# Hybrid decoder layer: operands of the recurrence through device memory, one forward substitution per head pair, low parts of weights on VectorE

## The chip, the cores and the metric

One core of a Trainium2 chip runs the program. The metric is the device time of one execution in microseconds; times given are medians of several executions. The engines are TensorE (PE in the profile; its weight loads are PEld), VectorE (DVE), ScalarE (ACT), GpSimd (POOL) and SyncE (SP), whose queue issues most DMAs. Each engine takes its instructions in the order of the program for that engine and waits on semaphores for the others.

## The reference

The layer takes x (1024 tokens, width 1024) through a SwiGLU feed-forward, a token mixer, a second feed-forward and a gated embedding, with layer norms between. Only the token mixer matters here, and of it the RWKV-7 half (512 columns, 8 heads of 64), which is a recurrence over the tokens:

```python
def _rwkv7_scan(r, w, k, v, kk, a):
    b_vec = kk * a
    def step(state, inp):
        r_t, w_t, k_t, v_t, kk_t, b_t = inp
        sa = jnp.einsum('bhvk,bhk->bhv', state, kk_t)
        state = (state * w_t[:, :, None, :] - sa[..., None] * b_t[:, :, None, :]
                 + v_t[..., None] * k_t[:, :, None, :])
        return state, jnp.einsum('bhvk,bhk->bhv', state, r_t)
    ...

def _token_mixer(hin, w_in, ...):
    z = jnp.einsum('bsd,dc->bsc', hin, w_in)
    z_ret, z_rw = z[..., :RET_COLS], z[..., RET_COLS:]
    ...
    ret = _retention_chunkwise(q, k, v)
    ret_out = jax.nn.silu(g) * _head_group_norm(ret, ret_gn_g, ret_gn_b, RET_GN_EPS)
    ...
    y = _rwkv7_scan(r_h, decay, k_h, v_h, kk, a)
    rw_out = (_head_group_norm(y, rw_gn_g, rw_gn_b, RWKV_GN_EPS) + bonus) * gate
    mixed = jnp.concatenate([ret_out, rw_out], axis=-1)
    return jnp.einsum('bsc,cd->bsd', mixed, w_out)
```

All of it is float32; large products are done as three products of split operands (a high part and a low part, `split`, lines 46 to 48, and `mm3`, lines 61 to 63).

## The kernel before

The mixer computes z in 31 column tiles of 128 (three of them before the stage, 28 in it: `z_tile`, 48 z products of 128x512 each, 1344 in all), stores them in device memory and takes the recurrence in chunks of 128 tokens. A unit is a pair of heads (u) and a half of the tokens (h): 8 units, each of 4 chunks of both heads, so 8 matrices of 128x128. For every unit:

- `rw_inputs` mixes neighbouring tokens, computes decays and the normalised key. On TensorE these are the products `wpw`, `apw`, `sspw`, `rnpw` and `bnpw`, on VectorE and ScalarE a chain between them.
- `rw_operands` (line 986) makes the operands `ar`, `bb`, `kp` and the matrices M1 (products `m1pw`, masked copies on line 1003), and the transposed `vt`, `bt`, `kt`. All of them stay in SBUF, in two buffers each.
- `substitution` (line 1015) inverts the 32 diagonal blocks of 32x32 of the unit: the matrices are written to device memory (1021), the blocks read back with a block per partition (1025, 32 partitions), and 31 steps of a product (1033) and a sum (1035) on VectorE work on all blocks at once. The result is written out (1037).
- `doublings` (line 1039) reads it back into the diagonal of `Xd` (1045), transposes it on VectorE (1047), and makes the inverse of 128x128 from it with the products `i1w` (1056) to `i5w`.
- `rw_chunks` runs the four chunks one after another: score products `scpw` (1099, 1102), masked copies on VectorE (1107, 1108), the products `chw` with two ScalarE copies between them, and the new state `wst` (1135). Then the group norm (`gstw`, `gnyw`, lines 797 to 805) and the output.

`retention` handles the other half of the heads (`vtpr`, `ktpr`, `rspr`, `kvpr`, `yor`). The z products of later pairs, and near the end the output projection (`w_out_group`, products `wopo`, 384 of them), are given as filler at low priority. In `z_tile` the low part of a weight is made on GpSimd (but for the first tile of the stage), in `w_out_operand` on GpSimd for every other operand.

The order of each engine's instructions is settled when the program is built: a list scheduler places them by priority (program order, moved by `high_priority`), so an instruction of low priority goes where its engine would otherwise be free; `issue_after(self.gate)` holds filler back until the matrix products that `gate` names. The loop of steps in `mixer` sets the program order:

```python
            for s in range(-1, 8):
                if s + 1 < 8:
                    self.rw_operands(W[s + 1])
                if s == -1:
                    self.lora(lor, 1)
                if s >= 0:
                    u, h = units[s]
                    self.doublings(W[s])
                    self.rw_chunks(W[s], mixed[4 + u])
                if s + 2 < 8:
                    W[s + 2] = inputs(s + 2)
```

Step s handles unit s; an odd step is the second half of the tokens of a pair.

## Time and profile before

| | us |
|---|---|
| median of 3 executions | 2357.45 (2352.09 to 2362.36) |
| profiled execution | 2365.46, span 2363.3 |
| TensorE busy | 2262.3 (96%) |
| VectorE busy | 1622.9 (69%) |
| ScalarE busy | 842.7 (36%) |
| GpSimd busy | 751.9 (32%) |
| recurrence stage | from 720 to 1564 of the span |
| first doublings of the steps 0 to 7 | 870, 923, 1016, 1078, 1198, 1260, 1379, 1437 |

The profile is of one execution, 8.0 us above the median. Busy time is the union of an engine's instructions; matmuls overlap one another, so a matmul's duration is longer than the distance to the next. "PEclk" is the granted TensorE clock as a share of full speed. Durations below are from this execution.

### The profile page before, as it was taken

What the parts mean: (1) busy time and instruction counts of PE and PEld (TensorE: products, weight loads), DVE (VectorE), ACT (ScalarE), POOL (GpSimd) and SP (SyncE); (2) the same over time, 40 slices, a digit from 0 to 9 for tenths busy, and PEclk for the clock granted to TensorE, in tenths of its full rate; (3) what the DMA queues carried; (4) which work ended last, traced back from release to release, by engine and by line L of the source; (5) the groups of instructions that cost most, each with busy time, mean ns of one, the idle gap of its engine ahead of it and who ended that gap; (6) DMA issues with size and microseconds to landing.
All of it is one profiled execution on the core that took longest, in us unless ns stands there. A gap on an engine that the chain in (4) does not pass through costs nothing.

```text
span 2363.3 us, 30893 instructions
## 1 busy us (share of the span) xinstructions
PE 2262.3 (96%) x10753; PEld 1818.2 (77%) x10753; DVE 1622.9 (69%) x2702; ACT 842.7 (36%) x1430; POOL 751.9 (32%) x614
## 2 busy tenths in 40 slices
PE   6999999999999899999899999988999999999999
PEld 5788888788786677777677777766888788788787
DVE  7677777665782487773864876679676767866862
ACT  4323232344643433322322322264323232445550
POOL 3336454300102323332432423225555453000220
PEclk9999999999999999999999999999999999999999
DMA  4345555497336343323333353322465544974321
GB/s 144 112 155 181 182 179 165 149 337 239 90 133 199 116 124 99 108 79 93 113 92 112 98 175 120 98 89 85 156 196 161 188 159 139 350 257 155 112 76 41
DMA packets 288945, 345.97 MB, mean 146 GB/s; under 512 B 35571, under 2 KB 162134, under 8 KB 288790
## 3 DMA queue, kind: packets, MB, share of 16 engines
q1 hardware_dynamic: 284208, 331.37, 43.6%
q0 software_dynamic: 3328, 12.06, 1.3%
q8 instruction: 85, 1.39, 0.2%
q10 hardware_dynamic: 1254, 0.58, 0.1%
q14 instruction: 70, 0.57, 0.1%
HBM read 237.50 MB, written 106.43 MB: 146 GB/s over the span
## 4 chain that ended last, share of the span: by engine, by line
PE 79%; DVE 14%; issue 2%; ACT 2%; DMA 1%; POOL 1%; SPq 0%; DVEq 0%; ACTq 0%; POOLq 0%
PE f1m L61 6%; PE f1m L62 6%; PE f1m L63 6%; PE f2m L61 5%; PE f2m L63 5%; PE f2m L62 5%; PE z L63 3%; PE z L61 3%; PE z L62 3%; DVE ixw L1035 2%; DVE itw L1033 2%; PE f1qa L62 1%; PE f1qa L61 1%; PE scpw L1099 1%; PE f1qa L63 1%
## 5 line engine op out<-in xcount | busy, mean ns | idle before, releaser
L63 PE MATMUL z<-x1Th,lo_win 128*128 128x512 f32 x448 | 191.3, 427 | 5.3 <-DVE lo_win L48 2.9
L61 PE MATMUL z<-x1Th,hi_win 128*128 128x512 f32 x448 | 191.1, 427 | 0.8 <-ACT hi_win L47 0.8
L62 PE MATMUL z<-x1Tl,hi_win 128*128 128x512 f32 x448 | 187.9, 420 | 0.0
L48 POOL TENSOR_TENSOR lo_win<-raw_win,hi_win 128x512 fp32r<-128x512 f32 x54 | 74.7, 1384 | 160.3 <-ACT hi_win L47 140.3
L1033 DVE TENSOR_TENSOR itw<-iltw,ixw 32x31 f32<-32x31 f32 (+15 forms) x248 | 104.5, 421 | 29.8 <-DMA iltw<-scrw 14.3
L1035 DVE TENSOR_TENSOR ixw<-ixw,itw 32x31 f32<-32x31 f32 (+15 forms) x248 | 108.9, 439 | 4.0
L63 PEld LDWEIGHTS z<-x1Th,lo_win 128*128 128x128 f32 x448 | 87.2, 195 | 26.4 <-POOL lo_win L48 4.0
L61 PEld LDWEIGHTS z<-x1Th,hi_win 128*128 128x128 f32 x448 | 87.5, 195 | 24.2 <-issue 3.8
L62 PEld LDWEIGHTS z<-x1Tl,hi_win 128*128 128x128 f32 x448 | 87.5, 195 | 20.3 <-issue 2.9
L149 POOL TENSOR_TENSOR f2tb<-f2tb,f2tb 128x512 f32<-128x512 f32 x44 | 71.9, 1634 | 91.5 <-DMA f2tb<-in_ffn_w_down 83.6
L48 DVE TENSOR_TENSOR f1hl<-f1s,f1hh 128x512 fp32r<-128x512 f32 x63 | 45.5, 723 | 61.6 <-ACT f1hh L47 61.6
L149 POOL TENSOR_TENSOR f1tb<-f1tb,f1tb 128x512 f32<-128x512 f32 x44 | 66.5, 1511 | 42.2 <-DMA f1tb<-in_ffn_w_down 35.7
L48 DVE TENSOR_TENSOR f2hl<-f2s,f2hh 128x512 fp32r<-128x512 f32 x63 | 44.8, 711 | 44.9 <-ACT f2hh L47 44.9
L47 ACT CAST f1hh<-f1s 128x512 fp32r<-128x512 f32 x63 | 39.2, 622 | 92.1 <-PE f1qa L62 42.3
L47 ACT CAST f2hh<-f2s 128x512 fp32r<-128x512 f32 x63 | 39.2, 623 | 89.8 <-PE f2qa L62 36.1
L659 ACT COPY zs<-z 128x512 f32<-128x512 f32 x56 | 32.7, 583 | 97.2 <-PE z L63 84.9
L108 DVE TENSOR_TENSOR f2S<-f2w 128x512 f32<-128x512 f32 x22 | 17.5, 800 | 72.1 <-DMA f2w<-in_ffn_w_gu 67.3
L47 ACT CAST hi_win<-raw_win 128x512 fp32r<-128x512 f32 x56 | 34.6, 619 | 90.2 <-PE z L62 82.2
L48 POOL TENSOR_TENSOR f1A12l<-f1w,f1A12h 128x512 fp32r<-128x512 f32 x22 | 30.9, 1408 | 106.8 <-ACT f1A12h L47 106.8
L62 PE MATMUL f2qa<-f2vl,f2hh 128*128 128x512 f32 x164 | 63.9, 390 | 0.5 <-DVE f2vl L48 0.5
L62 PE MATMUL f1qa<-f1vl,f1hh 128*128 128x512 f32 x164 | 63.9, 389 | 0.0
L63 PE MATMUL f2qa<-f2vh,f2hl 128*128 128x512 f32 x164 | 63.8, 389 | 0.0
(785 smaller groups left out, 7197.9 us busy)
## 6 DMA issues: line engine op xcount, KB each, us to landing
f1w<-in_ffn_w_gu SPq DMA_DIRECT2D x44, 512.0 KB
f2w<-in_ffn_w_gu SPq DMA_DIRECT2D x44, 512.0 KB
f1s<-hd SPq DMA_DIRECT2D x63, 256.0 KB
f2s<-hd SPq DMA_DIRECT2D x63, 256.0 KB
zs<-zs SPq DMA_DIRECT2D x56, 256.0 KB
raw_win<-in_w_in SPq DMA_DIRECT2D x54, 256.0 KB
f1tb<-in_ffn_w_down SPq DMA_DIRECT2D x44, 256.0 KB
wt<-f1tb SPq DMA_DIRECT2D x44, 256.0 KB
```

The source lines that it names most:

```text
L47: self.last_split = self.nc.scalar.copy(hi, src).ins
L48: (eng or self.nc.vector).tensor_tensor(out=lo, in0=src, in1=hi, op=ALU.subtract)
L61: mm(ps, a[0], b[0], start=first, stop=False)
L62: mm(ps, a[0], b[1], start=False, stop=False)
L63: mm(ps, a[1], b[0], start=False, stop=last)
L108: sub = lambda o, a, b, op=ALU.subtract: V.tensor_tensor(out=o, in0=a, in1=b, op=op)
L149: nc.gpsimd.tensor_tensor(out=t, in0=a, in1=b, op=ALU.subtract)
L659: nc.scalar.copy(zs, ps)
L1033: nc.vector.tensor_tensor(out=t, in0=lt[:, j, j + 1:].unsqueeze(2).broadcast_to([B, n, c]), in1=x[:, j:j + 1, 0:c].broadcast_to([B, n, c]) ...
L1035: nc.vector.tensor_tensor(out=x[:, j + 1:, 0:c], in0=x[:, j + 1:, 0:c], in1=t, op=ALU.add)
L1099: nc.tensor.matmul(ps[e][:, 0:2 * P], kp[rr, cs], ar[rr, c].rearrange("p a t -> p (a t)"), start=True, stop=True)
```

## The change

The operands of a unit (`ar`, `bb`, `kp`, `vt`, `bt`, `kt`) are written to a tensor in device memory, three of them by SyncE's queue and three by ScalarE's, and `rw_chunks` reads them back with one DMA for each chunk (448 KB, four buffers). The tiles in SBUF in which they are made, and M1, are single now; M1 is read back from device memory for the doublings. `substitution` takes the two units that follow an odd step (or both first units at the start) at once, 64 blocks on 64 partitions, and is called after the doublings of that odd step and before its chunks. `rw_inputs` and `rw_operands` of unit s + 2 come at the head of step s. The low parts of the weights of z and of the output projection are all made on VectorE.

```diff
@@ rw_operands
-        w.M1 = self.M1[w.h]
+        w.ops = self.dpool.tile([P, 4, 7, P], F32, tag="ops", name=f"ops{nm}", bufs=5)
+        w.L = self.dpool.tile([P, 8, P], F32, tag="scr", name=f"scr{nm}", bufs=5)
+        T = lambda tag, shape=[HALF], bufs=1: mb.tile([P] + shape, F32, tag=tag, name=f"{tag}{nm}", bufs=bufs)
...
-        self.substitution(w)
+        nc.sync.dma_start(w.L, self.M1)
...
-        toks = []
-        for t, x in (("vt", w.v), ("bt", w.bb), ("kt", w.kp)):
+        nc.sync.dma_start(w.ops[:, :, 2], c4(w.bb))
+        nc.sync.dma_start(w.ops[:, :, 0:2], w.ar)
+        nc.sync.dma_start(w.ops[:, :, 3], c4(w.kp))
+        for i, (t, x) in enumerate((("vt", w.v), ("bt", w.bb), ("kt", w.kp))):
             o = T("w" + t)
             nc.scalar.copy(o, self.transposes(x, f"{t}p{nm}"))
-            toks.append(o)
-        w.vt, w.bt, w.kt = toks
+            nc.scalar.dma_start(w.ops[:, :, 4 + i], c4(o))
@@ substitution
-    def substitution(self, w):
+    def substitution(self, ws):
...
-        scr = self.dpool.tile([P, 8, P], F32, tag="scr", name=f"scr{nm}", bufs=2)
-        nc.sync.dma_start(scr, w.M1)
-        lt = mb.tile([B, B, B], F32, tag="ilt", name=f"ilt{nm}", bufs=1)
-        for b in range(4):
-            bs = slice(B * b, B * b + B)
-            nc.sync.dma_start(lt[8 * b:8 * b + 8], scr[bs, :, bs].rearrange("i s j -> s i j"))
+        n_ = B * len(ws)
+        lt = mb.tile([n_, B, B], F32, tag="ilt", name=f"ilt{nm}", bufs=1)
+        for i, w in enumerate(ws):
+            for b in range(4):
+                bs = slice(B * b, B * b + B)
+                nc.sync.dma_start(lt[B * i + 8 * b:B * i + 8 * b + 8], w.L[bs, :, bs].rearrange("i s j -> s i j"))
...
-            nc.vector.tensor_tensor(out=t, in0=lt[:, j, j + 1:].unsqueeze(2).broadcast_to([B, n, c]),
-                              in1=x[:, j:j + 1, 0:c].broadcast_to([B, n, c]), op=ALU.mult)
+            nc.vector.tensor_tensor(out=t, in0=lt[:, j, j + 1:].unsqueeze(2).broadcast_to([n_, n, c]),
+                              in1=x[:, j:j + 1, 0:c].broadcast_to([n_, n, c]), op=ALU.mult)
             nc.vector.tensor_tensor(out=x[:, j + 1:, 0:c], in0=x[:, j + 1:, 0:c], in1=t, op=ALU.add)
...
@@ doublings
+        M1 = mb.tile([P, 8, P], F32, tag="M1", name=f"M1{nm}", bufs=1)
+        nc.sync.dma_start(M1, w.L)
@@ rw_chunks, for each chunk c
+            o = mb.tile([P, 7, P], F32, tag="ops", name=f"ops{nm}{c}", bufs=4)
+            nc.sync.dma_start(o, w.ops[:, c])
+            ar, (bb, kp, vt, bt, kt) = o[:, 0:2], [o[:, i] for i in range(2, 7)]
@@ w_out_operand
-            self.split(*parts, raw, self.nc.gpsimd if i else self.nc.vector)
+            self.split(*parts, raw)
@@ mixer
-                    self.z_tile(x1T, c0, zs[idx[c0]], *((nc.scalar, nc.vector) if early else (nc.sync, nc.gpsimd)))
+                    self.z_tile(x1T, c0, zs[idx[c0]], nc.scalar if early else nc.sync, nc.vector)
...
-                if s + 1 < 8:
-                    self.rw_operands(W[s + 1])
                 if s == -1:
+                    self.rw_operands(W[0])
                     self.lora(lor, 1)
+                if 0 < s + 2 < 8:
+                    W[s + 2] = inputs(s + 2)
+                    self.rw_operands(W[s + 2])
                 if s >= 0:
                     u, h = units[s]
                     self.doublings(W[s])
+                if s % 2 and s + 2 < 8:
+                    self.substitution([W[s + 1], W[s + 2]])
+                if s >= 0:
                     self.rw_chunks(W[s], mixed[4 + u])
-                if s + 2 < 8:
-                    W[s + 2] = inputs(s + 2)
```

Two places show what this does to the order of the engines.

TensorE at the start of the stage, the products of the second unit's inputs: before, z products (filler, lines 61 to 63) follow the last product of the decays, `apw`; 17 z products later comes `sspw` and then, with z products between them, `rnpw`, `bnpw` and `m1pw`.

```order
L931 MATMUL wpw_1_6870<-lor0w_1_6847,lorww_1_6849 128x512
L933 MATMUL apw_1_6872<-lor0w_1_6847,lorww_1_6849 128x512
L61 MATMUL z_0_6938<-x1Th,hi_win_0_6928 128x512
L62 MATMUL z_0_6938<-x1Tl_3698,hi_win_0_6928 128x512
L63 MATMUL z_0_6938<-x1Th,lo_win_0_6929 128x512
L61 MATMUL z_0_6938<-x1Th,hi_win_0_6928 128x512
L62 MATMUL z_0_6938<-x1Tl_3699,hi_win_0_6928 128x512
L63 MATMUL z_0_6938<-x1Th,lo_win_0_6929 128x512
```

The same place after (`gps` are the last gate products of `lora`):

```order
L782 MATMUL gps_1_6743<-ld_1_6715,gupzk_6721 128x512
L933 MATMUL apw_1_6774<-lor0w_1_6749,lorww_1_6751 128x512
L965 MATMUL sspw_1_6803<-ones,sqw_1_6801 128x2 x4
L812 MATMUL rnpw_1_6814<-ident,rbw_1_6812 128x128 x4
L980 MATMUL bnpw_1_6824<-rkw_1_6822,ones 128x512
L1001 MATMUL m1pw_10_6835<-arw_1_6830,bbw_1_6832 128x128 x3
L1001 MATMUL m1pw_11_6836<-arw_1_6830,bbw_1_6832 128x128 x3
L1001 MATMUL m1pw_10_6835<-arw_1_6830,bbw_1_6832 128x128
L1001 MATMUL m1pw_11_6836<-arw_1_6830,bbw_1_6832 128x128
L61 MATMUL z_0_6997<-x1Th,hi_win_0_6987 128x512
```

The z products have moved behind the whole chain. Up to the first `i1w` of the stage 432 z products stand in the order before and 370 after; 192 and 130 of them come after `apw`.

VectorE, before, in the chunks of step 0: the substitution of the next unit (`itw`, `ixw`) alternates with the masked copies of the scores (`scz`) and the state (`wst`).

```order
L1107 COPY_PREDICATED scz_6353<-mask,scpw_010_9093 128x256
L1033 TENSOR_TENSOR itw_115_8926<-iltw_1_8873,ixw_1_8878 32x256
L1108 COPY_PREDICATED scz_6353<-mask,scpw_010_9093 128x128
L1035 TENSOR_TENSOR ixw_1_8878<-ixw_1_8878,itw_115_8926 32x16x16
L1131 TENSOR_SCALAR wst_6361<-chw_00_9075,few_0_7682 64x64
L1033 TENSOR_TENSOR itw_116_8929<-iltw_1_8873,ixw_1_8878 32x255
L1131 TENSOR_SCALAR wst_6361<-chw_00_9075,few_0_7682 64x64
L1035 TENSOR_TENSOR ixw_1_8878<-ixw_1_8878,itw_116_8929 32x15x17
```

After, at the end of the chunks of step 1, where the substitution of units 2 and 3 begins (the steps have lines 1035 and 1037 now):

```order
L1144 SCALAR_TENSOR_TENSOR wst_6359<-chw_12_8392,few_1_6794,sfw_121_8407 64x64
L797 TENSOR_REDUCE gstw_1_8444<-yrw_1_8305 128x8
L798 TENSOR_SCALAR gstw_1_8444<-gstw_1_8444 128x8
L799 TENSOR_TENSOR gnyw_1_8445<-yrw_1_8305,gstw_1_8444 128x512
L802 TENSOR_REDUCE gstw_1_8444<-gsqw_1_8449 128x8
L804 RECIPROCAL gstw_1_8444<-gstw_1_8444 128x8
L805 TENSOR_TENSOR gnyw_1_8445<-gnyw_1_8445,gstw_1_8444 128x512
L1035 TENSOR_TENSOR itw_00_8210<-iltw_0_8198,ixw_0_8207 64x31
L1037 TENSOR_TENSOR ixw_0_8207<-ixw_0_8207,itw_00_8210 64x31
L1035 TENSOR_TENSOR itw_01_8213<-iltw_0_8198,ixw_0_8207 64x60
L1037 TENSOR_TENSOR ixw_0_8207<-ixw_0_8207,itw_01_8213 64x30x2
```

The steps stand behind the chunks and the group norm of an odd step, and nothing of them stands in the chunks of any step. On TensorE, 136 z products stood between the last chunk of each of the steps 1, 3 and 5 and the next `i1w`; now there are 139, 150 and 134, and the products `m1pw` of the next unit (and, in steps 3 and 5, `sspw`, `rnpw` and `bnpw`) have left this stretch for the chunks.

## Rows read from the trace of the kernel before

**Rows 1.** Stage windows: length, busy PE, PEld, DVE, ACT, POOL, PEclk, DMA share, GB/s.

```profile
720.00:870.30 150.30, 136.51 (x560) 97.90 (x559) 68.60 (x135) 57.69 (x93) 46.97 (x63) 0.97 0.47 146
870.30:1564.00 693.70, 660.09 (x3706) 519.87 (x3704) 480.46 (x1075) 207.03 (x398) 233.94 (x226) 0.96 0.35 108
```

**Rows 2.** Windows of the three stretches after an odd step's last chunk.

```profile
964.50:1015.80 51.30, 47.98 (x234) 38.08 (x234) 39.43 (x95) 15.81 (x27) 18.70 (x17) 0.93 0.48 143
1138.50:1197.80 59.30, 52.70 (x250) 41.32 (x249) 44.46 (x89) 19.49 (x34) 28.14 (x22) 0.91 0.39 117
1321.40:1379.10 57.70, 51.67 (x248) 41.44 (x247) 45.08 (x89) 17.90 (x31) 28.11 (x21) 0.91 0.40 117
```

**Rows 3.** Windows of two even steps.

```profile
1015.80:1077.90 62.10, 57.72 (x327) 45.93 (x326) 44.67 (x105) 17.92 (x38) 26.31 (x26) 0.95 0.26 78
1197.80:1259.80 62.00, 57.58 (x334) 45.05 (x333) 47.57 (x106) 16.86 (x36) 26.28 (x28) 0.97 0.33 99
```

**Rows 4.** Groups of the substitution: count, busy us, mean ns, idle before.

```profile
L1033 DVE TENSOR_TENSOR itw<-iltw,ixw 32x31 f32<-32x31 f32 (+15 forms) x248 | 104.5, 421 | 29.8 <-DMA iltw<-scrw 14.3 <-POOL csw L941 11.7
L1035 DVE TENSOR_TENSOR ixw<-ixw,itw 32x31 f32<-32x31 f32 (+15 forms) x248 | 108.9, 439 | 4.0
```

**Rows 5.** Timeline, step 3's tail: start us, us, engine, line, operation.

```profile
1151.30 0.41 DVE L1035 TENSOR_TENSOR ixw<-ixw,itw 32x256 f32<-32x256 f32 x1
1151.46 2.00 POOL L975 TENSOR_TENSOR wkw<-wkw,kfw 128x512 f32<-128x512 f32 x1 [3.12 <-DVE kkw L974]
1152.24 1.50 DVE L1033 TENSOR_TENSOR itw<-iltw,ixw 32x255 f32<-32x255 f32 x1
```

**Rows 6.** Timeline, from step 1's last chunk to step 2's first doubling.

```profile
964.22 0.39 PE L1143 MATMUL chw<-saw,scz 128*128 128x64 f32 x2
1005.01 0.18 DVE L1035 TENSOR_TENSOR ixw<-ixw,itw 32x31 f32<-32x31 f32 x1
1005.40 0.32 SPq L1037 DMA_DIRECT2D scsw<-ixw  x1
1007.59 1.78 SPq L1045 DMA_DIRECT2D Xd<-scsw  x4
1015.53 0.39 PE L63 MATMUL z<-x1Th,lo_win 128*128 128x512 f32 x1
1015.76 0.94 PE L1056 MATMUL i1w<-Xd,M 128*128 128x128 f32 x7
```

**Rows 7.** Timeline, the second unit's inputs.

```profile
808.16 0.69 PE L933 MATMUL apw<-lor0w,lorww 64*128 64x512 f32 x1
815.08 1.05 PE L965 MATMUL sspw<-ones,sqw 128*128 128x2 f32 x8 [1.63 <-ACT sqw L962]
824.43 1.46 PE L980 MATMUL bnpw<-rkw,ones 128*128 128x512 f32 x2 [2.13 <-DVE rkw L978]
829.78 0.72 DVE L1003 COPY_PREDICATED M<-mask,m1pw 128x512 f32<-128x512 uint8 x1
```

**Rows 8.** Timeline, SyncE queue between first unit's matrix and its substitution.

```profile
801.09 0.33 SPq L1021 DMA_DIRECT2D scrw<-M  x1
804.75 1.51 SPq L1025 DMA_DIRECT2D iltw<-scrw  x4
```

**Rows 9.** Source line L1056, first step: duration ns, first and last start.

```profile
L1056 PE MATMUL i1w<-Xd,M x16: 272/275/275, 870.6 to 872.2; 128*128 128x128 f32 x16
```

**Rows 10.** Source line L48 in the stage, GpSimd and VectorE.

```profile
L48 POOL TENSOR_TENSOR lo_win<-raw_win,hi_win x54: 1256/1294/3362, 735.1 to 1377.7; 128x512 fp32r<-128x512 f32 x54
L48 POOL TENSOR_TENSOR mw<-wo,mw x16: 1263/1293/1730, 1410.3 to 1542.7; 128x512 fp32r<-128x512 f32 x16
L48 DVE TENSOR_TENSOR lo_win<-raw_win,hi_win x2: 673/677/681, 720.7 to 725.8; 128x512 fp32r<-128x512 f32 x2
```

**Rows 11.** Timeline, a DMA issued by ScalarE.

```profile
705.49 0.41 ACTq L52 DMA_DIRECT2D raw_win<-in_w_in  x1
```

**Rows 12.** DMA issues: KB each, median us to landing.

```profile
x<-xacc POOLq DMA_DIRECT2D x8, 512.0 KB, 2.9
```

More of the change, by code (lines that the diff above doesn't have):

```diff
@@ L714, in mixer_setup @@
         nc.vector.tensor_copy(self.mask, m.rearrange("p (a b) -> p a b", a=2))
-        self.M1 = [c.tile([P, 8, P], F32, name=f"M1{i}") for i in range(2)]
+        self.M1 = c.tile([P, 8, P], F32, name="M1")
         self.Xd = c.tile([P, 8, P], F32, name="Xd")
-        for t in self.M1 + [self.Xd]:
+        for t in (self.M1, self.Xd):
             nc.gpsimd.memset(t, 0.0)
@@ L1055, in doublings @@
             for i in range(4):
-                nc.tensor.matmul(ps[:, i * P:(i + 1) * P], w.M1[:, 4 * q + i], self.Xd[:, 4 * q + i], start=True, stop=True)
+                nc.tensor.matmul(ps[:, i * P:(i + 1) * P], M1[:, 4 * q + i], self.Xd[:, 4 * q + i], start=True, stop=True)
             pm = mb.tile([P, 4, P], F32, tag="ipm", name=f"ipm{nm}{q}", bufs=2)
@@ L1071, in doublings @@
         for i in range(8):
-            nc.tensor.matmul(ps[hi, 64 * i:64 * i + 64], w.M1[lo, i, hi], X64[lo, i], start=True, stop=True)
+            nc.tensor.matmul(ps[hi, 64 * i:64 * i + 64], M1[lo, i, hi], X64[lo, i], start=True, stop=True)
         pm = mb.tile([P, 8, 64], F32, tag="ipm", name=f"ipn{nm}", bufs=2)
@@ L1084, in rw_chunks @@
         sl = slice(h * HALF, (h + 1) * HALF)
-        ar, bb, kp, vt, bt, kt, XT, fe = w.ar, w.bb, w.kp, w.vt, w.bt, w.kt, w.XT, w.fe
+        XT, fe = w.XT, w.fe
         yr = self.ring("c", f"yr{nm}")
@@ L1098, in rw_chunks @@
                 rr = slice(64 * e, 64 * e + 64)
-                nc.tensor.matmul(ps[e][:, 0:2 * P], kp[rr, cs], ar[rr, c].rearrange("p a t -> p (a t)"), start=True, stop=True)
+                nc.tensor.matmul(ps[e][:, 0:2 * P], kp[rr], ar[rr].rearrange("p a t -> p (a t)"), start=True, stop=True)
             for e in range(2):
                 rr = slice(64 * e, 64 * e + 64)
-                nc.tensor.matmul(ps[e][:, 2 * P:3 * P], bb[rr, cs], ar[rr, c, 1], start=True, stop=True)
+                nc.tensor.matmul(ps[e][:, 2 * P:3 * P], bb[rr], ar[rr, 1], start=True, stop=True)
             E = []
@@ L1112, in rw_chunks @@
             if not first:
-                nc.tensor.matmul(ch[:, 0:P], ar[:, c, 0], st, start=True, stop=False)
+                nc.tensor.matmul(ch[:, 0:P], ar[:, 0], st, start=True, stop=False)
             for e in range(2):
-                vs = slice(c * P + 64 * e, c * P + 64 * e + 64)
+                vs = slice(64 * e, 64 * e + 64)
                 nc.tensor.matmul(ch[:, 64 * e:64 * e + 64], E[e][:, 0], vt[:, vs], start=first, stop=first or e == 1)
@@ L1124, in rw_chunks @@
             if not (h == 1 and c == 3):
-                nc.tensor.matmul(ch[:, 2 * P:3 * P], kt[:, cs], vt[:, cs], start=True, stop=False)
-                nc.tensor.matmul(ch[:, 2 * P:3 * P], bt[:, cs], sa, start=False, stop=True)
+                nc.tensor.matmul(ch[:, 2 * P:3 * P], kt, vt, start=True, stop=False)
+                nc.tensor.matmul(ch[:, 2 * P:3 * P], bt, sa, start=False, stop=True)
                 for e in range(2):
@@ L1137, in rw_chunks @@
             if not first:
-                nc.tensor.matmul(ch[:, Y:], ar[:, c, 1], st, start=True, stop=False)
+                nc.tensor.matmul(ch[:, Y:], ar[:, 1], st, start=True, stop=False)
             for e in range(2):
-                vs = slice(c * P + 64 * e, c * P + 64 * e + 64)
+                vs = slice(64 * e, 64 * e + 64)
                 es = slice(Y + 64 * e, Y + 64 * e + 64)
```

21 lines of the change are left out of this document (11 added, 10 removed).

## The prediction

> **What bounds the kernel now.** First the table of stages. The change touches the recurrence stage alone, from 720 to 1564 us. In its eight steps (870.3 to 1564) TensorE is busy 660.1 of 693.7 us, VectorE 480.5, GpSimd 233.9, ScalarE 207.0, DMA 0.35 [rows 1]: TensorE bounds it, idle for 33.6 us, and its granted clock of 0.96 takes another 0.04 x 693.7 = 28 us. So 61 us of these steps are stall and 632 are work at full clock.
>
> Then the same table by step, to see where the stall lies. The "tail" of an odd step runs from its last chunk to the next step's first doubling. The three tails that have a next substitution in them last 51.3, 59.3 and 57.7 us, with 3.3, 6.6 and 6.0 idle and clocks of 0.93, 0.91 and 0.91 that cost 3.6, 5.3 and 5.2: 30.0 us of stall, half of all, over 44.4 + 47.4 + 46.5 = 138.3 us of work [rows 2]. Two even steps show 7.5 and 6.3 us of stall by the same sum [rows 3]. In the second and third tail VectorE is busy 44.5 and 45.1 us, and the timeline shows what with: substitution steps, with everything else of VectorE between them. TensorE goes in order, so a tail lasts as long as the longer of two things: its own queued work, and VectorE's way to the first doubling's operand.
>
> **The change part by part.**
>
> *Four substitutions instead of eight.* One has 62 instructions and takes (104.5 + 108.9) / 8 = 26.7 us [rows 4]; four fewer take 106.7 us from VectorE. The new ones have 64 partitions and as many elements on each. I take the same duration, since an instruction of 128 partitions and 512 elements takes 0.68 us [rows 10] and the longest step, 32 x 256, 0.41 [rows 5]; the other end, twice the time, would leave VectorE where it is. Undisturbed, a step takes 0.18 (shortest) to 0.41 us (longest) [rows 5, 6], some 20.3 us for 62; so 6.4 us of 26.7 are disturbance. One step shows it: 1.50 us instead of 0.41 while GpSimd multiplies [rows 5].
>
> The Trainium skill, page "SBUF — State Buffer", section "SBUF: two separate sides", says that VectorE and GpSimd share a port pair as an exclusive lock, held for a whole instruction. The trace agrees: that step grew by 1.1 us beside a 2.00 us product.
>
> *The start.* In the new order of TensorE nothing stands between the second unit's input products and its matrix; the z products that filled this stretch come after. The matrix must now be there before the one substitution can begin. In the trace the chain from the `apw` product (808.2) to the copied matrix (830.5) takes 22.3 us [rows 7], with substitution steps and a z copy in it; without them I take 18, between 16 (up to the last input product, 824.4) and 22. Then: matrix out and blocks back, 801.1 to 806.3, and 2 to land, 7 us [rows 8]; the run, 20.3 and some 6.5 of other work between (four low parts of 0.68, z products' rotation, mixing), 27 us; out and back again 6.3 us (write issued 1005.4, reads issued until 1009.4, and 2.2 to land as the write took) [rows 6]. From 809.5 this ends at 868, where the first doubling stands at 870.6 now [rows 9]. But 130 z products lie before it in place of 192, and each takes 0.23 us [rows 6]: 62 x 0.23 = 14.3 us of work is left for later, less 2.8 for the earlier doubling: **+11.5 us**, between +8 and +17.
>
> *The tails.* No chunk has substitution steps in it any longer; the whole run stands in the odd tail, behind the group norm. Today's way in the first tail: last chunk product ends at 964.6, last substitution step at 1005.2, operand back at 1011.6, so 47.0 us [rows 6] (TensorE came to the doubling only at 1015.8, having z products to do). New in it: the seven shortest steps, which stood before the tail (+1.6), four low parts (+2.7), the group norm ahead of the run instead of among it (+2.6, an estimate: four passes of 0.67). Gone: two matrix copies of 0.72 [rows 7], and half of the disturbance, since GpSimd loses its low parts (-3.2). That gives 49; a wait of VectorE for the retention products should shrink too, so I take 48, between 43 (no disturbance, waits gone) and 53 (all added, none gone). TensorE's own tail work: the z products go from 136 each to 139, 150 and 134 (+3.5 us), the matrix products and three transposes move into the chunks (16 + 12 instructions at 0.107 [rows 9], 3.0 us per tail), and in two tails the products of the next inputs (2.2 us: 1.05 for the sums of squares [rows 7], the rest alike). So 42.1, 45.4 and 40.8 us of work: all below 48. The tails take 144 instead of 168.3 us, -24.3; the 10.0 us of work that left them is done in the chunks: **-14.3 us**.
>
> *Chains of the inputs* now run among the doublings and chunks of all steps. Today they cost 7.5 and 6.3 in even steps [rows 3] and little in odd chunks, which are full of z products. I take 3 to 4 us for each of six, as much as goes: **0**, between -8 and +8.
>
> *Operands through device memory.* Per unit SyncE issues eight DMAs more (three operands, four chunk loads, the matrix) at 0.32 us [rows 6], 2.6 us in a queue in which z stores and weight loads stand behind; ScalarE issues three at 0.41 [rows 11], 9.8 us in all, beside copies that the chunks wait for. ScalarE is 70% idle; I take **+1**, between 0 and +9.8. The traffic is 33 MB on some 75 (108 GB/s over 694 us), which takes the DMA share from 0.35 to 0.50. A chunk load of 448 KB lands in about 2.9 us (512 KB do) [rows 12] and four buffers let it be asked for a chunk ahead: nothing. The single matrix buffer costs a wait of 3.7 us for its write [rows 8], covered by the 18 us between the first two units and a step between later ones.
>
> *Low parts on VectorE.* 54 and 16 instructions of 1.29 us leave GpSimd (90.5 us), 70 of 0.68 go to VectorE (47.6) [rows 10]. Those in the tails are counted above; the others lie under TensorE's work: 0. Between -6, if half the disturbance of the other instructions goes as well, and +6, if z products wait behind VectorE's queue.
>
> **Sum:** 11.5 - 14.3 + 0 + 1 = -1.8 us. VectorE gets 59 us lighter and TensorE hardly notices. The profiled execution took 2365.46 us (span 2363.3), so 2363.7 by it; it lies 8 us above the median of 2357.45, to which the same difference gives **2355 us**.
>
> **Rivals.** (1) *Faster, 2333 us.* The way through VectorE takes 43 us; the tails are then 43, 45.4 and 43, -26.9 with the moved work, the start costs 8 and the chains give back 5: -24. For it: 6.4 us of disturbance per run, and GpSimd's lighter queue. Against: all retention products of GpSimd stay in the tails.
>
> (2) *Slower, 2380 us.* The pair's run is late in every tail: 53 us, so that the tails give nothing (159 + 10 against 168.3), the start costs 17 and the chains 5: +23. It decides from 52.5 us on (+11.8 in all at the other terms' values). For it: the run can't start before the group norm, and TensorE has nothing else queued before the doubling. Against: today's 47.0.
>
> (3) *Slower by the port, 2371 us.* The moved low parts hold GpSimd up where a chain goes through it: three products a unit (the exponents' argument, k, k times the decay), 24 x 0.68 = 16 us. GpSimd's 2.00 us for the k product [rows 5] speaks for it; that GpSimd has 90 us less to do, against. The Trainium skill's rule on the lock, named above, reads this way too: whichever starts first holds the other off.
>
> (4) *The chunk loads are not ahead*, their buffers coming free too late: 32 x 2.9 = 93 us, 2448. Nothing in the order speaks for it.
>
> **How the numbers follow.** A measurement of this kernel can tell about 0.5%, 11.8 us, from no change. No change: 0.38. Faster (1): 0.34, since the bounds of the tails and the start go further down than up. Slower: (2) 0.19, (3) 0.06, (4) 0.03, together 0.28. The forecast's own range is 2346 to 2368; with (1) and (2) down to their middles, 2328 to 2382, leaving out the rarer ends of (1) and (2) and all of (4).
>
> **What would show it.** Right: the first doubling within 866 to 873 us with TensorE idle some 10 us on each side of the second matrix; the substitution's two groups at 124 instructions each and a mean near 0.38 us; the three tails at 46 to 50 us with TensorE idle before the doubling; no wait of the chunk products on a DMA. Wrong: tails without idle time (1), tails above 52 us (2), longer k products on GpSimd (3), score products that wait for operand loads (4). The argument falls if the time outside 720 to 1564 us moves by more than 5 us.

## The result and the profile after

The changed kernel takes **2385.94 us** (median of 4, 2384.05 to 2393.63) against 2359.9 for the kernel before in the same comparison: ratio 1.012, 95% interval 1.008 to 1.016. It is 26 us slower, outside the forecast range (2328 to 2382). The profiled execution, the longest of the four, has a span of 2391.8 us; behind the recurrence stage lie 800.5 us against 798.2 before, so the loss lies in the stage, which takes 871.3 us against 845.1.

The stage's rows, before the first doubling and from there to the end, with the columns of [rows 1]:

```profile
720.00:872.10 152.10, 127.20 (x497) 90.15 (x498) 65.81 (x133) 53.91 (x87) 23.53 (x45) 0.90 0.56 176
872.10:1590.00 717.90, 683.03 (x3766) 533.60 (x3765) 418.99 (x898) 214.59 (x407) 139.53 (x163) 0.93 0.46 144
```

VectorE went from 480 to 419 us and GpSimd from 234 to 140, as the diff says. TensorE's clock fell to 0.90 and 0.93, where [rows 1] has 0.97 and 0.96. The three odd tails and the two even steps that answer to [rows 2, 3], and the substitution's two groups that answer to [rows 4]:

```profile
986.20:1038.00 51.80, 46.67 (x209) 36.44 (x208) 40.77 (x94) 16.34 (x27) 8.79 (x10) 0.90 0.57 180
1163.90:1216.90 53.00, 48.38 (x219) 38.38 (x219) 41.55 (x97) 17.51 (x28) 8.94 (x10) 0.94 0.54 168
1345.30:1397.70 52.40, 42.61 (x199) 34.16 (x198) 41.23 (x93) 13.61 (x22) 10.69 (x8) 0.87 0.53 158
1038.00:1085.20 47.20, 45.60 (x307) 35.70 (x306) 28.40 (x61) 16.22 (x35) 12.56 (x18) 1.00 0.46 138
1216.90:1269.90 53.00, 50.62 (x310) 40.56 (x309) 29.20 (x58) 16.63 (x36) 11.51 (x16) 0.90 0.42 126
```

```profile
L1037 DVE TENSOR_TENSOR ixw<-ixw,itw 64x31 f32<-64x31 f32 (+15 forms) x124 | 52.2, 421 | 3.2
L1035 DVE TENSOR_TENSOR itw<-iltw,ixw 64x31 f32<-64x31 f32 (+15 forms) x124 | 48.1, 388 | 12.4 <-DMA lorww<-in_rw_a_up 9.4
```

Half as many steps, on 64 partitions, at nearly the old duration each (405 ns on average against 430): 113 us left VectorE, where 106.7 were forecast. The tails are 3.7 us shorter on average (157.2 against 168.3 us in all), but their idle time and what the clock costs in them, by the sum that the prediction made of [rows 2], are 34.7 us against 30.0.

One sum makes all kernels comparable. I cut the stage into windows of 4 us; in each, TensorE's busy time times its granted clock is *work*, busy time times the rest is *half clock*, and what is not busy is *idle*. Idle and half clock together are the *stall*. For the kernel before this gives 764.7 us of work and 80.4 of stall from 720 us to the stage's end, for the changed one 756.9 and 114.4, in a second profile of it 759.3 and 109.3. The stall's places (us; the variants are told of below):

| profiled kernel | start | steps 0, 2, 4 | steps 1, 3, 5 | steps 6, 7 | stall | work |
|---|---|---|---|---|---|---|
| before | 18.7 | 15.5 | 31.4 | 14.8 | 80.4 | 765 |
| changed | 34.5 | 13.3 | 37.7 | 28.9 | 114.4 | 757 |
| changed, again | 36.0 | 9.5 | 41.3 | 22.4 | 109.3 | 759 |
| low_only | 20.8 | 43.3 | 39.5 | 12.1 | 115.7 | 764 |
| dram_only | 36.5 | 15.5 | 29.6 | 8.0 | 89.5 | 776 |
| dram_pool | 19.4 | 15.5 | 38.8 | 7.1 | 80.7 | 777 |
| order_back | 27.4 | 10.4 | 21.2 | 11.6 | 70.7 | 773 |
| low_back | 37.1 | 27.4 | 51.6 | 4.1 | 120.4 | 760 |
| gate0 | 33.8 | 18.1 | 44.8 | 5.5 | 102.4 | 758 |
| half | 34.2 | 8.2 | 52.9 | 18.6 | 113.7 | 773 |
| rows0 | 35.1 | 14.3 | 44.3 | 15.5 | 109.4 | 768 |
| ops_pool | 26.4 | 27.5 | 21.4 | 4.6 | 79.9 | 761 |
| ops_gate | 21.7 | 5.4 | 29.0 | 23.0 | 79.0 | 763 |
| ops_low | 31.4 | 21.3 | 58.4 | 17.2 | 128.5 | 763 |

The work of these kernels is the same within 20 us, the stall differs by 58. A difference in work under some 15 us is not read: two profiles of one kernel differ by 2, but the same products give 765 and 777 in kernels of other orders. Work and stall add up to the length of the stage, so what the sum wrongly counts as work is missing from the stall: the stage of half is 15 us longer than that of the changed kernel, at the same stall.

So the changed kernel has 29 to 34 us more stall, and 5 to 8 less work: 16 to 17 of stall at the start, 8 to 14 in the last pair, 6 to 10 in the odd steps, less 2 to 6 in the even ones. The order of TensorE's instructions in gate0 is the changed kernel's from the first doubling on, and there the odd steps have 44.8 and the last pair 5.5: between executions of one order these places differ about as much as they do between the two kernels. The start does not (34.5 and 36.0).

**The start.** Two windows of 10 us, of before and then of the changed kernel:

```profile
810.00:820.00 10.00, 8.37 (x42) 6.58 (x41) 2.98 (x9) 5.83 (x11) 2.53 (x4) 1.00 0.23 74
840.00:850.00 10.00, 10.00 (x44) 8.04 (x44) 9.41 (x19) 2.53 (x5) 2.69 (x3) 1.00 0.43 127
```

```profile
810.00:820.00 10.00, 2.98 (x12) 2.50 (x12) 4.00 (x6) 3.25 (x5) 3.27 (x4) 0.56 0.00 0
840.00:850.00 10.00, 2.83 (x7) 0.92 (x5) 9.48 (x20) 3.23 (x5) 2.76 (x2) 0.76 0.85 279
```

The first gap was forecast: nothing fills the second unit's chain. The second, at 840 us, is a wait of 6.4 us for a weight's high part, whose load is late (who waits, for whom; us, times, longest):

```profile
PE z L61 <- ACT hi_win L47: 6.4, 1, 6.4
```

SyncE's issues in both kernels (start, duration, queue, line, operation, out<-in), before and then changed:

```profile
827.52 0.33 SPq L982 DMA_DIRECT2D bv<-rkw  x1
827.89 0.43 SPq L830 DMA_DIRECT2D zkr<-zs  x1
828.42 0.40 SPq L660 DMA_DIRECT2D zs<-zs  x1
830.52 0.32 SPq L1021 DMA_DIRECT2D scrw<-M  x1
830.94 0.39 SPq L52 DMA_DIRECT2D raw_win<-in_w_in  x1
```

```profile
823.04 0.34 SPq L982 DMA_DIRECT2D bv<-rkw  x1
823.42 0.53 SPq L1010 DMA_DIRECT2D opsw<-bbw  x1
824.06 0.62 SPq L1011 DMA_DIRECT2D opsw<-arw  x1
...
828.95 4.11 SPq L1027 DMA_DIRECT2D iltw<-scrw  x4
833.10 0.51 SPq L920 DMA_DIRECT2D lorww<-in_rw_a_up  x1
833.74 1.13 SPq L1051 DMA_DIRECT2D M1w<-scrw  x1
834.98 1.86 SPq L1097 DMA_DIRECT2D opsw<-opsw  x4
...
843.42 1.03 SPq L52 DMA_DIRECT2D raw_win<-in_w_in  x2
```

From the bonus store (`bv`) to the next weights' load (`raw_win`) there are 3.4 us before and 20.4 now. The Trainium skill, page "DMA: Bandwidth & Descriptors", section "Issuing engines are not separate DMA queues", says that spreading DMAs over engines saves only the time to initiate them, usually small beside the transfer. Here the issues take some 11 of the 20.4 us, and the queue's head waits for another 7.7: for `apw`, a landing and the second matrix.

**The odd tails.** TensorE's waits in the first and the second (who waits, for whom; us, times, longest):

```profile
PE ktpr L812 <- POOL zkr L837: 2.6, 1, 2.6
PE vtpr L812 <- DMA zvr<-zs: 2.0, 1, 2.0
PE rspr L855 <- DVE kdr L845: 0.4, 1, 0.4
```

```profile
PE rspr L855 <- DVE kdr L845: 3.8, 1, 3.8
PE ktpr L812 <- POOL zkr L837: 0.8, 1, 0.8
```

All of it is the retention's; the third tail has 8.3 us of the same waits, 1.1 at `ytpw` and 0.4 at a z product. No wait stands at the doubling in any of the three. Before, the second tail's two longest waits are these:

```profile
PE rnpw L812 <- ACT rbw L971: 4.0, 1, 4.0
PE rspr L855 <- DVE kdr L845: 1.0, 1, 1.0
```

The third has 4.0 at `rnpw` too. So over the three tails the 8.0 us of waits for the next inputs are gone, and those of the retention went from 8.1 to 17.9. Three queues that go in order lie behind them. The first is SyncE's; in the first tail:

```profile
971.69 2.56 SPq L1027 DMA_DIRECT2D iltw<-scrw  x4
987.39 0.34 SPq L660 DMA_DIRECT2D zs<-zs  x1
...
989.96 0.42 SPq L834 DMA_DIRECT2D zksr<-zs  x1
990.43 0.41 SPq L841 DMA_DIRECT2D zvr<-zs  x1
```

The z store (L660) waited 13.0 us at the queue's head for its tile, and the retention's last loads behind it. The last load that GpSimd's rotation of k needs (`zksr`) is issued 3.8, 4.6 and 3.8 us after the last chunk product; before, it was 23, 1.6 and 2.1 us ahead of it. On GpSimd the rotation (`zkr`) then stands behind two products of the chunks' output (`wow`, 2.6 to 2.7 us). On VectorE the product `kdr` stands behind steps of the substitution, 1.7, 4.1 and 3.0 us after its operand is there (1.3, 2.0 and 2.0 before); the second tail (start, us, engine, line, operation):

```profile
1178.58 1.16 PE L855 MATMUL rspr<-zqr,zkr 64*128 64x128 f32 x8
1182.36 0.41 DVE L1037 TENSOR_TENSOR ixw<-ixw,itw 64x247 f32<-64x247 f32 x1
1182.80 0.69 DVE L845 TENSOR_TENSOR kdr<-ktpr,kdec 128x512 f32<-128x512 f32 x1
1183.54 0.79 PE L855 MATMUL rspr<-zqr,zkr 64*128 64x128 f32 x2 [3.81 <-DVE kdr L845]
```

**The last pair.** Two windows among the chunks of steps 6 and 7, of the changed kernel and then of gate0, a variant (below) whose instructions have the same order there:

```profile
1417.70:1427.70 10.00, 10.00 (x36) 7.50 (x36) 1.91 (x6) 0.72 (x3) 0.88 (x2) 0.50 0.32 88
1467.70:1477.70 10.00, 10.00 (x40) 7.95 (x40) 4.27 (x11) 4.25 (x8) 2.15 (x3) 0.50 0.23 78
```

```profile
1427.40:1437.40 10.00, 10.00 (x67) 7.93 (x68) 2.82 (x9) 1.59 (x6) 1.76 (x4) 1.00 0.71 225
1467.40:1477.40 10.00, 10.00 (x68) 8.20 (x66) 8.11 (x19) 2.46 (x8) 6.01 (x5) 1.00 0.67 199
```

TensorE is busy throughout in both, with 36 to 40 products in one and 67 in the other: the clock is at 1.2 GHz or at 2.4.

### The profile page after: what moved, and what is told of

It reads as the page before. It is cut to its first block, busy times and chain, and to the rows that moved or that the text cites. A ratio compares the mean times of both kernels' runs of the same rounds, so it can differ in the third digit from the quotient of the medians.

```text
span 2391.8 us, 30775 instructions
## 1 busy us (share of the span) xinstructions
PE 2274.9 (95%) x10753; PEld 1823.5 (76%) x10753; DVE 1558.6 (65%) x2524; ACT 849.5 (36%) x1434; POOL 636.0 (27%) x535
## 4 chain that ended last, share of the span: by engine, by line
PE 80%; DVE 11%; DMA 3%; issue 3%; ACT 2%; POOL 1%; SPq 0%; ACTq 0%; DVEq 0%; POOLq 0%
PE f1m L61 6%; PE f1m L62 6%; PE f1m L63 6%; PE f2m L61 5%; PE f2m L63 5%; PE f2m L62 5%; PE z L63 3%; PE z L61 3%; PE z L62 3%; PE f1qa L62 1%; PE f1qa L61 1%; PE f1qa L63 1%; PE scpw L1108 1%; PE pg L62 1%; PE pg L61 1%
## 5 line engine op out<-in xcount | busy, mean ns | idle before, releaser
L48 DVE TENSOR_TENSOR f1hl<-f1s,f1hh 128x512 fp32r<-128x512 f32 x63 | 45.5, 723 | 61.7 <-ACT f1hh L47 61.7
L48 DVE TENSOR_TENSOR lo_win<-raw_win,hi_win 128x512 fp32r<-128x512 f32 x56 | 39.9, 718 | 66.1 <-ACT hi_win L47 58.1
L48 DVE TENSOR_TENSOR f2hl<-f2s,f2hh 128x512 fp32r<-128x512 f32 x63 | 44.8, 711 | 44.6 <-ACT f2hh L47 44.6
L47 ACT CAST f2hh<-f2s 128x512 fp32r<-128x512 f32 x63 | 39.2, 623 | 87.8 <-PE f2qa L62 35.1
L1143 POOL TENSOR_SCALAR sfw<-wst,few 64x64 f32<-64x64 f32 x48 | 24.0, 500 | 150.7 <-DVE wst L1144 100.1
L179 DVE TENSOR_TENSOR f1U<-f1m,f1U 128x512 f32<-128x512 f32 x50 | 33.5, 687 | 46.8 <-PE f1m L63 46.8
L63 PE MATMUL f1qa<-f1vh,f1hl 128*128 128x512 f32 x164 | 63.8, 389 | 0.0
L61 PE MATMUL f1qa<-f1vh,f1hh 128*128 128x512 f32 x164 | 63.3, 389 | 0.0
```

The costliest lines, as they stand in the source:

```text
L47: self.last_split = self.nc.scalar.copy(hi, src).ins
L48: (eng or self.nc.vector).tensor_tensor(out=lo, in0=src, in1=hi, op=ALU.subtract)
L61: mm(ps, a[0], b[0], start=first, stop=False)
L63: mm(ps, a[1], b[0], start=False, stop=last)
L179: add = lambda out, a, b, eng=V: eng.tensor_tensor(out=out, in0=a, in1=b, op=ALU.add)
L1143: nc.gpsimd.tensor_scalar(out=sf[rr], in0=st[rr, rr], scalar1=fe[rr, c:c + 1], scalar2=None, op0=ALU.mult)
```

## The experiments

Ratios are to the kernel before, with 95% intervals. First theory: the order (start, tails, last pair without filler) costs the time. Rivals: the operands' way through device memory; the low parts on VectorE.

**Each part alone, or taken back.** *dram_only*: the step order of before and one substitution a unit, low parts on GpSimd.

```
+                if s + 1 < 8:
+                    self.rw_operands(W[s + 1])
+                    self.substitution([W[s + 1]])
                 if s == -1:
-                    self.rw_operands(W[0])
                     self.lora(lor, 1)
...
-                if s % 2 and s + 2 < 8:
-                    self.substitution([W[s + 1], W[s + 2]])
...
```

> The operands of each unit pass through device memory (and the matrix through one buffer), while the step order, the eight single substitutions and the low parts on GpSimd are those of the kernel before. Theory (the loss of the changed kernel comes from the new order: the start, the odd tails and the last pair): 2360 us, within 6 us of before, tails of the odd steps 50 to 60 us as before, no score product waiting for a chunk load for more than 1 us. Rival (device memory: 33 MB more traffic, eleven more DMA issues a unit on SyncE and ScalarE): 2375 us or more, with the chunks of each step longer by 1 to 2 us.

2380.69 us, 1.008 (1.005 to 1.011): by its time the rival is right. Its start has the changed kernel's second gap. The step order is that of before, but the list that the scheduler makes of it for TensorE is not: 384 z products stand ahead of the first doubling, before 432.

```profile
840.00:850.00 10.00, 2.30 (x10) 1.50 (x8) 9.21 (x24) 0.00 (x0) 0.00 (x0) 0.75 0.96 336
```

*low_only*: the kernel before with the change's two lines on the low parts.

```
-                    self.z_tile(x1T, c0, zs[idx[c0]], *((nc.scalar, nc.vector) if early else (nc.sync, nc.gpsimd)))
+                    self.z_tile(x1T, c0, zs[idx[c0]], nc.scalar if early else nc.sync, nc.vector)
...
-            self.split(*parts, raw, self.nc.gpsimd if i else self.nc.vector)
+            self.split(*parts, raw)
```

> The kernel before with the low parts of the weights on VectorE and nothing else changed. Theory: 2360 us within 6 us; GpSimd has 90 us less to do, VectorE 48 more, nearly all beside TensorE. Rival (low parts on VectorE lengthen the way of the substitution in the tails and hold z products up): 2372 us or more, tails 3 us longer each.

2398.63 us, 1.016 (1.012 to 1.020), more than the whole change; the theory fails here. The order changed with the edit: the scheduler puts fewer z products among the chunks (17 and 9 in steps 1 and 2, before 21 and 40). The chunks of these steps:

```profile
943.80:992.20 48.40, 47.10 (x256) 37.07 (x256) 28.77 (x60) 13.74 (x29) 12.89 (x17) 0.75 0.21 63
1042.40:1091.00 48.60, 44.47 (x223) 37.51 (x222) 29.98 (x82) 9.06 (x22) 10.29 (x13) 0.64 0.08 25
```

Before, the same two stretches take 41.2 and 40.5 us at a clock of 0.96 and 0.97: the loss in these stretches is half clock.

*low_back*: the same two lines the other way round in the changed kernel.

> The changed kernel with the low parts back on GpSimd. Theory: 2386 us within 6 us of the changed kernel: about four low parts of 0.68 us leave each tail's way through VectorE (2.7 us), GpSimd's products stretch the substitution's steps again by about as much. Rival (low parts on VectorE are the cost): 2368 us or less, tails 48 us instead of 52.

2395.93 us, 1.015 (1.010 to 1.020): beside pairs, low parts on VectorE save some 10 us (the intervals overlap), against both views. *order_back*: dram_only with the low parts on VectorE.

> The changed kernel with the step order and the eight single substitutions of before; operands through device memory on SyncE and low parts on VectorE stay. Theory (the two other parts cost on their own 20 and 37 us, and the substitution for pairs takes back what the low parts put on VectorE): 2405 us or more, 20 over the changed kernel. Rival (the new order and the pairs are a cost of their own): 2375 us or less.

2380.38 us, 1.003 (1.000 to 1.007); its times fall into two groups, 2357 to 2367 and 2380 to 2393, and the profile is of the first. Both expectations miss. The parts don't add up: 37 and 20 us alone, 8 by the ratio together, and the new order with its pairs adds some 16 to 20 us to that.

**SyncE's queue.** *gate0*: the start's filler waits for the first unit's products.

```
                     self.rw_operands(W[0])
+                    gate0 = self.gate
...
-                with self.tc.issue_after(self.gate):
+                with self.tc.issue_after(self.gate if s >= 0 else gate0):
```

> The changed kernel, where the filler z products at the start wait for the first unit's matrix products instead of the second's. Theory (in the changed kernel TensorE idles and its clock falls to half between 805 and 870 us, since no filler may run beside the second unit's chain): 2374 us, 8 to 16 us less than the changed kernel; the z products stand among the second unit's products, the granted clock of 805 to 870 us is near 1, and the first doubling stays within 872 to 880 us with less work left behind it. Rival (the chain of the second unit sets the start, and the z products in its way delay it as long as they take): 2386 us within 5, the first doubling 8 to 14 us later.

2382.32 us, 1.009 (1.006 to 1.012): the rival by time, though the first doubling is no later (871.8 us). The filler now runs from 810 to 820 us (7.96 busy), and TensorE then waits from 830 to 850 for the same late weights (4.6 of 20 busy). *dram_pool*: dram_only with five transfers on GpSimd (the first and the last of them):

```
-        nc.sync.dma_start(w.ops[:, :, 2], c4(w.bb))
+        nc.gpsimd.dma_start(w.ops[:, :, 2], c4(w.bb))
...
-            nc.sync.dma_start(o, w.ops[:, c])
+            nc.gpsimd.dma_start(o, w.ops[:, c])
```

> The operands pass through device memory in the step order of before, with single substitutions and the low parts on GpSimd; the operand writes of SyncE, the matrix's load and the chunk loads are issued by GpSimd in place of SyncE. Theory (device memory costs through SyncE's queue alone: 20 us with the transfers on SyncE): 2361 us within 6, 432 z products before the first doubling, as before, and no idle TensorE of over 3 us between 835 and 860 us. Rival (the traffic of 33 MB or the waits for landings cost): 2375 us or more, as with SyncE issuing.

The gap is gone, 432 z products stand ahead of the first doubling and the start's stall is back at 19.4 us (before 18.7), but the time is not: 2383.15 us, 1.008 (1.006 to 1.011).

```profile
840.00:850.00 10.00, 7.84 (x34) 6.04 (x33) 9.52 (x17) 2.52 (x4) 4.09 (x4) 1.00 0.50 156
```

*wq_pool*: only the z weights' loads on GpSimd.

```
-                    self.z_tile(x1T, c0, zs[idx[c0]], nc.scalar if early else nc.sync, nc.vector)
+                    self.z_tile(x1T, c0, zs[idx[c0]], nc.scalar if early else nc.gpsimd, nc.vector)
```

> The changed kernel, where the loads of the z products' weights are issued by GpSimd instead of SyncE. Theory (at the start SyncE's queue holds the weight loads up: it waits for the second unit's bonus product, then issues operand writes, block loads and chunk loads for 20 us, and the next weights are asked for at 843 us in place of 831, so that TensorE idles 6 to 9 us and then runs at the half clock): 2370 us, 10 to 20 less than the changed kernel's 2386, no idle TensorE of over 3 us between 830 and 860 us. Rival (the second unit's own chain of input products sets the start, not a queue): 2386 us within 6, the idle time stays between 840 and 850 us.

2391.55 us, 1.012 (1.008 to 1.016): no gain, the start's stall is 36.8 us. No high part is waited for at the start now, but the z store stands in the same queue: SyncE waits for `apw`, the store is issued behind it, and TensorE waits for the copy that needs the stored tile's buffer:

```profile
SPq L919 <- PE apw L933: 8.5, 1, 8.5
PE z L61 <- ACT zs L659: 4.2, 1, 4.2
```

So the queue holds this start up by another transfer, which neither view had. *ops_pool*: the changed kernel with the five transfers of dram_pool on GpSimd.

> The changed kernel, where the three operand writes of SyncE, the matrix's load and the chunk loads are issued by GpSimd; the weight loads stay on SyncE. Theory (SyncE's queue is what the operands through device memory cost): 2370 us or less, as for the weight loads on GpSimd. Rival A (the traffic itself or the landing times cost): 2386 us within 6. Rival B (GpSimd, which goes in order too, now holds the chunks up): 2395 us or more, with score products waiting for operand loads.

**2360.88 us, 0.999 (0.996 to 1.001): the whole loss is gone**, the stall is 79.9 us. Its three odd tails show no wait for `zkr`, `zvr` or `kdr`; the first has only these:

```profile
PE sspw L965 <- ACT sqw L962: 0.3, 1, 0.3
PE yor L872 <- POOL zqr L860: 0.3, 1, 0.3
```

The last `zksr` load is issued 11 to 34 us ahead of the last chunk product here, and `kdr` starts within 0.8 us of its operand. But the scheduler made another list for TensorE as well: 441 z products stand ahead of the first doubling, in the changed kernel 370, and no step has the same order. What the queue's waits cost and what the order costs is not separated by this run.

Three arrangements of the rest with these transfers on GpSimd. *ops_gate*: with gate0's edit. *ops_low*: with low_back's. *ops_order*: with the step order of before.

> The changed kernel with the operand transfers issued by GpSimd, where the filler at the start waits for the first unit's matrix products instead of the second's. Theory (with SyncE's queue free the gate is what is left of the start's loss, 9 us of idle and half-clock time between 805 and 830 us): 2352 us, 5 to 12 less than the 2361 with the transfers on GpSimd alone. Rival (the start's order is shuffled and the loss comes back in the next chunks): 2361 us within 5.

> The changed kernel with the operand transfers issued by GpSimd and the low parts on GpSimd too. Theory (beside pairs, low parts on VectorE save about 10 us, since VectorE has room there and GpSimd's chains don't wait): 2371 us, 10 over the 2361 with the operand transfers on GpSimd alone. Rival (low parts on VectorE cost here as well as in the kernel before): 2350 us or less.

> The changed kernel with the operand transfers issued by GpSimd and the step order and single substitutions of before. Theory (with SyncE's queue free the pairs give nothing that single substitutions don't): 2361 us within 8, 432 z products before the first doubling and under 16 us of idle TensorE there. Rival (the pairs are worth what they take off VectorE, some 20 us): 2380 us or more.

2360.88 us (1.000, 0.997 to 1.004), 2415.83 (1.021, 1.016 to 1.025) and 2388.68 (1.010, 1.007 to 1.013). The first and the last come out as their rivals said, *ops_low* above both views. In ops_gate the gate takes 5 us of stall from the start, and the last pair loses 23.0 in place of 4.6 in this profile, with the same order of TensorE there. With these transfers on GpSimd, the new step order with pairs beats the old one with single substitutions by 28 us, and low parts on VectorE beat those on GpSimd by 55, each in an order of its own.

*zst_act* and *zst_before*: ScalarE issues the z stores, in the changed kernel and in the one before.

```
-            nc.sync.dma_start(dst[:, sl], zs)
+            nc.scalar.dma_start(dst[:, sl], zs)
```

> The changed kernel, where ScalarE, which copies each z tile, also issues its store, in place of SyncE; the operands' transfers stay on SyncE. Theory (stores that wait in SyncE's queue for their tile hold up the loads behind them: 13.0 us in the first odd tail, where the retention's products then wait 4.7 us, and the weight loads at the start): 2365 us, within 8, the waits of the retention's products in each odd tail under 2 us. Rival (the number of issues and the traffic cost, not the waiting stores): 2386 us within 5.

> The kernel before with the z stores issued by ScalarE. Theory (before, SyncE's queue has no operand transfers behind these stores, so little waits): 2361 us within 6. Rival (the stores hold up this kernel as much): 2345 us or less, faster than both kernels.

2376.97 us, 1.005 (1.003 to 1.008): 9 us back of 26, between the two views. The waiting stores may be part of the loss; with 415 z products ahead of the first doubling the order is another one here too. Its profile is of its longest execution (2411 us) and its times are not read. The other: 2413.38 us, 1.022 (1.018 to 1.025), where neither view expected a loss: before's order is disturbed by it as by low_only (51.6 us of stall in steps 0, 2 and 4).

**The tails and the last pair.** *half*: every second step of the substitution left out.

```
-        for j in range(B - 1):
+        for j in range(0, B - 1, 2):
```

> The changed kernel with every second step of the substitution left out (16 of 31, so that the inverse is not the reference's); all else stays. Theory (in the odd tails the way through VectorE sets the time, 52 us against 41 to 45 us of TensorE's work): each of three tails becomes 42 to 46 us, the start 6 to 8 us shorter, with the work of filler products moved behind: 2360 us, between 2350 and 2370. Rival (the filler is all that counts; what the tails give back is taken by chunks without filler): 2380 us or more, the tails shorter but the chunks of the next steps longer by as much.

2416.02 us, 1.022 (1.017 to 1.026). The tails shrank as expected; two of them:

```profile
1175.80:1213.20 37.40, 28.61 (x142) 22.98 (x142) 28.81 (x59) 11.11 (x18) 10.49 (x10) 0.86 0.48 142
1364.80:1400.70 35.90, 28.02 (x142) 23.08 (x142) 27.69 (x57) 10.15 (x17) 9.19 (x7) 0.86 0.49 144
```

Their idle time did not shrink (8.8 and 7.9 us, in the changed kernel 4.6 and 9.8), and nearly all of it lies at the retention's products (`rspr` waits 7.4 us for `kdr` in the first of these two). The z products that had filled the tails (139, 150, 134) are 78, 75 and 78 and stand among chunks instead. `kdr` still stands behind substitution steps, 7.6 and 6.7 us after its operand. A shorter substitution shortens the tails and moves filler about; it does not make the kernel faster. Why this one is 30 us slower at an unchanged stall is open: its work reads 16 us higher.

*rows0*: the output products are not put back. *pad67*: 16 products added in steps 6 and 7.

```
                     for ks, halves in rows.get(s, ()):
-                        with self.tc.high_priority(offset=FILLER):
+                        with self.tc.high_priority(offset=0):
```

```
+            if u == 3:
+                pd = self.ptile("ta", f"pd{nm}{c}", 2)
+                for i in range(2):
+                    nc.tensor.matmul(pd, self.ident, o[:, 0:4].rearrange("p a t -> p (a t)"), start=True, stop=True)
```

> The changed kernel, where the output products of the last three steps are no longer put 300 places back, so that 97 of them stand among the last step's chunks instead of 22. Theory (the last two steps' chunk chains run with 48 filler products, TensorE's clock falls to the half level there, and the last pair takes 192 us where it took 185 before): 2378 us, 5 to 12 less than the changed kernel, with the granted clock above 0.9 in the last step's chunks. Rival (the chain of chunks sets these steps at any clock, and filler only lengthens them): 2386 us within 5.

> The changed kernel with two more products of 128 x 512 (f32, their result is read by nothing) in each chunk of the last two steps, 16 in all, about 0.5 us each or 8 us of added work. Theory (TensorE's clock falls to the half level in these chunks because their products leave it little to do, and that costs 17 to 24 us of the changed kernel): 2376 us, 10 less than the changed kernel in spite of the added work, and the granted clock of the last two steps' chunks at 0.95 or more. Rival (the chain of the chunks sets these steps, the clock only follows): 2394 us, 8 more.

2390.22 us (1.011, 1.008 to 1.014) and 2397.51 (1.014, 1.011 to 1.018): the rivals by time. In rows0 the last step has no half clock, but step 6 still has 10.2 us. In pad67 both steps keep it:

```profile
1420.00:1430.00 10.00, 10.00 (x36) 7.84 (x36) 1.43 (x5) 0.80 (x3) 0.88 (x2) 0.50 0.17 48
```

*after_again*: the changed kernel unedited.

> The changed kernel once more, for a second profile. Theory (TensorE's clock falls to the half level where its chunk chains run with few filler products, so that the place is the kernel's own): 2386 us within 5, and the chunks of the last two steps lose 15 us or more to the clock again. Rival (which chunks lose the clock changes from execution to execution): the same time within 8, with the last two steps' chunks near 1.0 and the loss elsewhere or absent.

2391.98 us, 1.010 (1.007 to 1.013); steps 6 and 7 lose 8.5 us each to the clock, 10.2 and 13.6 in the first profile, and gate0 nothing with the same order there. In this order the loss came in two profiles of three. *ops_pad_all*: one such product in every chunk, beside ops_pool.

> The changed kernel with the operand transfers issued by GpSimd, and one more product of 128 x 512 (f32, its result is read by nothing) in each chunk of all steps, 32 in all, 16 us of added work. Theory (35 us of half clock are left in the chunks' chains with the transfers on GpSimd, and some filler in each chunk keeps the clock up): 2352 us, the half clock's cost under 15 us. Rival (the added work costs more than the clock gives back): 2370 us or more.

2390.63 us, 1.010 (1.007 to 1.013). Half clock fell from 35.1 to 20.0 us, and the work rose from 761 to 787: a loss. No variant beats both kernels; ops_pool and ops_gate equal the one before.

## Why the prediction was wrong

**The step that failed is "The tails", −14.3 us.** It took a tail to last as long as the longer of TensorE's queued work and "VectorE's way to the first doubling's operand", and priced that way at 48 us. In its own sum the term measured +4.7: the tails last 157.2 us in place of 144, and 15.8 us of work left them in place of 10.0. That is 19 of the 28 us between forecast and result. The length did follow VectorE's way: the last read of the operand is issued at 1034.4, 1213.6 and 1393.5 us, 48 to 50 us after the last chunk product and 3 to 4 ahead of the doubling; with the 2 us to land that the prediction took from [rows 6], the way is some 51 us in place of 48. But TensorE waits nowhere at the doubling, because filler covers the way. It waits for the retention's inputs, 17.9 us in place of 8.1, and for these waits the prediction had no term. `half` shows that a tail can lose 15 us and the kernel gain nothing. A tail's length was the wrong quantity; its stall was in [rows 2], and TensorE's list of waits for these rows names the retention and the next inputs, and never the doubling.

**"Operands through device memory", +1 (0 to 9.8), failed too.** Issues were counted (2.6 us a unit) and not what they stand ahead of: 20.4 us from the bonus store to the weights' load. dram_only has 18 us more stall at the start and 20 us more time, in an order that changed with it; dram_pool shows that the start's part comes from SyncE's queue. ops_pool shows that with the transfers off SyncE the whole change costs nothing, by the queue and by the order that it leads to together. In the old step order the same move gains nothing (dram_pool 19 us over before, ops_order 25): why is open, and the 12 us by which their work reads higher than before's can't be resolved by this sum.

**The start, +11.5 (8 to 17), was right in size**: 16 to 17 us of stall, the first doubling at 872.1 us in the forecast 866 to 873, idle on both sides of the second matrix. In part that is luck: only the first gap is the filler's gate; the second is the queue's, which this term did not have, and gate0 shows that mending the one feeds the other.

**The chains of the inputs, 0**: the even steps had 2 to 6 us less stall, within ±8. **The low parts, 0 (±6)**: alone 37 us lost, in an order that changed with them, with pairs 10 us gained; no single number for them exists. **The last pair** was not in the sum at all: it had 8 to 14 us more stall, by the clock. Since gate0 has 5.5 us there in the same order, before 14.8, it is not shown that the change causes this. Why the clock falls in some executions and not in others of the same order is not settled.

Rival (2) named 2380 us, tails of 53 and a start of 17, nearest to the result; but its reason, a doubling that TensorE waits for, is in no tail, and `half` speaks against it. For (3) the k products on GpSimd would be longer; their median is 1.69 us, before 1.70. No score product waited for an operand load (4).

## What to carry to other kernels

Where one engine is busy nearly all the time, sum its idle time and its low clock before and after, place by place, and ask what it waits for in each; a stretch made shorter may only move filler. When DMAs are added to a queue that goes in order, list what stands behind them and what its head waits for. In a kernel whose order a scheduler sets, try each part alone: here the parts cost 37 and 20 us apart and, once the transfers had left SyncE's queue, nothing in the new step order but 19 to 25 us in the old. Compare the engines' lists too, since here the edit of one queue changed them all.

## What was not expected of the hardware

TensorE's granted clock stood at half for some 20 us at a time while the engine was busy in every window (10.00 of 10.00, 36 narrow products), and the same order ran at full clock with 67 in another kernel. The Trainium skill, page "TensorE: Matmul & The Clock Gate", section "HAM oscillation — how this bites in real kernels", ties the loss to idle gaps of TensorE; the profile shows none over 0.7 us in these stretches or in the 15 us ahead of them, though its ends of products are modelled. Products of 128 x 512 in f32 added to these chunks did not raise the clock (0.50 in the row above).
